# Residue-order q split straight from PSUM, and a later expected landing of transfers, in a hybrid decoder layer

## The chip, the cores and the metric

The kernel runs on one core of a Trainium2 chip. The metric is the time of one execution in device microseconds; the figure for a kernel is the median of its runs. TensorE is called PE in the rows, VectorE DVE, ScalarE ACT, GpSimd POOL, and SyncE, which issues all the DMAs of this kernel, SP. All arithmetic is fp32; a matrix product is made of three passes over operands that are each split into a high and a low part in fp32r.

## The reference

One decoder layer over 1024 tokens of width 1024. Cut to what matters here:

```python
a = rmsnorm(h, ln_pre_mix)
q, k, v, u, z = split(a @ w_in)             # 3 x 512 columns for attention, 2 x 512 for gating
attn = dilated_attention(q, k, v)           # 8 heads of 64; (window, dilation) = (128,1), (512,4), (2048,16)
sgu = spatial_gating(u, z, ...)             # chunks of 128 tokens
h = h + rmsnorm(concat(rmsnorm(attn), rmsnorm(sgu)) @ w_out)
g, up = split(rmsnorm(h) @ w_gate_up)       # 2 x 2816 columns
h = h + rmsnorm((silu(g) * up) @ w_down)
h = h + sigmoid(h @ w_pe_gate + b_pe_gate) * (p @ w_pe_proj)
```

In the attention q is scaled by 64 ** -0.5. A query sees the tokens of its own neighbourhood, and farther ones only at a distance that is a multiple of four, so the far part of the second half of the sequence (tokens 512 to 1023, which look back into tokens 0 to 511) splits into four residues of the position modulo four.

## The kernel before, in words

**Order of the program.** The kernel does not issue its instructions as they are written. Every operation is recorded in a graph (`Graph.call`; all share one source line in the profile, L383), priced (`price`) and put in order by `order` (line 224): a list scheduler that keeps, for each engine, a time at which it is free, and starts the earliest written operation whose inputs are ready in the plan and whose buffers are free. Buffers are of four kinds: M (4 KB a partition, 47 of them), S (2 KB, 14), T (small, 28) and P (the eight PSUM banks, with limits by group: three for scores, two for the weighted sums, two for transposes, two for fill work). For PE an input from another engine counts as sure only after a margin of 0.25 us. Reads of a PSUM bank are ordered like writes, so two engines never read one bank at once. The instructions are then issued in the picked order, and each engine runs its own list in that order. A DMA is planned at lines 326 to 331: it starts 0.4 us after its issue or when the one before has moved its bytes, takes its bytes at 330 KB per us (`load` has a `rate` that divides this, for transfers in small pieces), ends a fixed time later, and no more than eight are in flight.

**Stages.** The products use a two-level block scheme of seven block products (`in_products`; numbers 1, 2, 6, 5, 3, 7, 4 in this order for q and k). In order of time: norm and transposes of x with the V projection, then z and u with the gating unit, then q and k, to about 221.5 us; attention for four pairs of heads, first half and then second half of the sequence, mixed with fill work (the output projection of the gating part, the p embeddings, and the first two block products of 20 column blocks of the feed-forward: `gated`, `ple`, `first_products`), to about 475; the rest of gate/up, the down projection and the last gate, to the end.

**Around the change.** After block product 2, four PSUM banks hold, added to what product 1 left, q of the first half of the sequence, feature-major: 128 features (two heads) by 512 tokens. After product 4, the last, the four banks hold q of the second half. `q_out` (line 763) scales a bank into a high part (ScalarE `mul`) and a low part (VectorE `scalar_tensor_tensor`: scaled source minus high part), both in one M tile, and stores it to DRAM (`q_low`, `q_high`). For the second half it also makes a copy `turned` in which the 512 tokens are regrouped by residue modulo four: two ScalarE copies, one of each part, which read the M tile at a step of four elements and write it contiguously; a second DMA stores it as `q_far`. The attention loads these back with the two heads stacked differently: `stacked_q` (line 807), `prepare_low` (line 813, six loads a pair) and `prepare_high` (line 820, twelve loads a pair). `prepare_high` for a pair is recorded behind step 2 of the pair before, and for the first pair in the last pair's first half.

`far_unit` makes the scores of the four residues, a softmax, transposes and a weighted sum for one head; its ScalarE copy out of the `av` bank reads PSUM at a step of 128 elements. `unit` does the same for a pair of near query blocks. In both, `softmax` is a VectorE pass that adds the bias and takes the row maximum (CUSTOM_DVE_ANT_0 in the rows), then a ScalarE exponential.

Of the kernel before, what the change touches and what calls it, by code (L numbers as in the profile page):

```python
# [12 lines left out]
F32R = mybir.dt.float32r  # L13
# [4 lines left out]
P = 128  # L18
# [5 lines left out]
HD = 64  # L24
# [8 lines left out]
LO, HI = slice(0, 512), slice(512, 1024)  # L33
ADD, SUB, MUL = ALU.add, ALU.subtract, ALU.mult
# [79 lines left out]
class Graph:  # L114
# [109 lines left out]
    def order(self):  # L224
# [19 lines left out]
        port, dma, table, lanes = 0.0, 1.5, 0, [0.0] * 8  # L244
# [37 lines left out]
        def pick(e, now):  # L282
            best = None
            front = ops[first]
            for rank, i in waiting[e][: self.LOOK[e]] + [(front.rank, first)] * ((front.rank, first) in waiting[e]):
                o = ops[i]
                if o.port[e] and port > now + 1e-9:
                    continue
                if best is not None and o.sure > now:
                    continue  # L290
                if not fits(o, now):
                    continue
                if e != "tensor" or o.sure <= now:
                    return o
                best = o
            return best
# [6 lines left out]
        while left:  # L303
            if not events:
                raise ValueError(f"stuck at {ops[first].what} {first}")
            now = heapq.heappop(events)
            while events and events[0] <= now + 1e-9:
                heapq.heappop(events)
            while coming and coming[0][0] <= now + 1e-9:
                _, rank, i, e = heapq.heappop(coming)  # L310
                if ops[i].start is not None:
                    continue
                bisect.insort(waiting[e], (rank, i))
            for e in engines:
                if at[e] > now + 1e-9 or not waiting[e]:
                    continue
                o = pick(e, now)
                if o is None:
                    continue
                busy, took = o.cost[e]  # L320
                o.start, o.engine = now, e
                picked.append(o)
                if o.table and o.table != table:
                    busy, took, table = busy + 1.4, took + 1.4, o.table
                at[e] = now + busy
                if e == "sync":
                    dma = max(dma, now + 0.4) + o.bytes / 330e3
                    o.end = dma + 1.7
                    lanes = lanes[1:] + [o.end]
                    at[e] = max(at[e], lanes[0])  # L330
                else:
                    o.end = now + took
                if o.port[e]:
                    port = o.end
                    heapq.heappush(events, port)
                for x in o.engines:
                    if (o.rank, o.i) in waiting[x]:
                        waiting[x].remove((o.rank, o.i))
                o.new = [b for b in o.bufs if b.slot is None]
                for b in o.new:  # L340
                    b.slot = heapq.heappop(free[b.kind])[1]
                    group[b.group] = group.get(b.group, 0) + 1
                    b.ahead = first
                    early[b.kind][first : b.born] += 1
                for b in o.bufs:
                    b.left -= 1
                    b.until = max(b.until, o.end)
                    if not b.left:
                        heapq.heappush(free[b.kind], (b.until, b.slot))
                        group[b.group] -= 1  # L350
                        live[b.kind][b.born : b.last + 1] -= 1
                        early[b.kind][b.ahead : b.born] -= 1
                        heapq.heappush(events, b.until)
                done[o.i] = True
                left -= 1
                while first < n and done[first]:
                    first += 1
                for u in o.users:
                    u.waits -= 1
                    if not u.waits:  # L360
                        release(u)
                heapq.heappush(events, at[e])
                heapq.heappush(events, now + 0.02)
# [25 lines left out]
def hybrid_block(ctx: ExitStack, tc, a, out):  # L389
    G = Graph()  # L390

    def M(dt=F32, shape=(P, 1024), group=None):
        return G.buf("M", shape, dt, group)
# [13 lines left out]
    def DR(shape):  # L407
        return G.buf("D", shape)
# [4 lines left out]
    def dve(what, **kw):  # L413
        return G.call("vector", what, **kw)

    def load(dst, src, rate=1.0):
        o = G.call("sync", "dma_start", dst, src)
        o.bytes /= rate
        return o

    def tt(dst, x, y, op=ADD, engines="vector"):
        return G.call(engines, "tensor_tensor", out=dst, in0=x, in1=y, op=op)

    def copy(dst, src):
        return G.call("scalar", "copy", dst, src)
# [174 lines left out]
    x = a["x"][0]  # L600
# [137 lines left out]
    for q, banks in in_products(2048, 1536, zu_mm):  # L738
        for i in range(4):
            if q in (1, 6, 5):  # L740
                v, t = {1: (zs, i), 6: (us, i), 5: (us, i + 4)}[q]
# [5 lines left out]
            else:  # L747
                v = {2: zs, 3: us}.get(q, us)[i + 4 * (q == 7)]
# [10 lines left out]
    q_low, q_high, q_far = ([DR([P, 2, 512]) for _ in range(4)] for _ in range(3))  # L759
    k_all = [DR([P, 2, S]) for _ in range(4)]  # L760
    q_part, k_part = [SM() for _ in range(4)], [M(F32, (P, 2, 512)) for _ in range(4)]

    def q_out(src, dsts):
        hl = M(F32R, (P, 2, 512))
        G.call("scalar", "mul", hl[:, 0], src, HD**-0.5)
        dve("scalar_tensor_tensor", out=hl[:, 1], in0=src, scalar=HD**-0.5, in1=hl[:, 0].f32(), op0=MUL, op1=SUB)
        load(dsts[0], hl.f32())
        if len(dsts) > 1:
            turned = M(F32R, (P, 2, 512))
            for j in range(2):  # L770
                copy(turned[:, j].split(P), hl[:, j].f32().then(lambda v: v.rearrange("p (s c) -> p c s", c=4)))
            load(dsts[1], turned.f32())

    def k_out(src, cs, i):
        hl = M(F32R, (P, 2, 512))
        split(hl[:, 0], hl[:, 1], src)
        load(k_all[i][:, :, cs], hl.f32())
# [5 lines left out]
    for q, banks in in_products(0, AW, qk_mm, (1, 2, 6, 5, 3, 7, 4)):  # L783
        for i in range(4):
            dst = {1: q_part[i], 2: q_part[i], 6: k_part[i][:, 0], 3: k_part[i][:, 0], 5: k_part[i][:, 1],
                   7: k_part[i][:, 1], 4: None}[q]
            if q in (1, 6, 5):
                copy(dst, banks[i])
            elif q != 4:
                tt(dst, banks[i], dst)  # L790
            if q == 2:
                q_out(dst, [q_low[i]])
            if q == 4:
                q_out(banks[i], [q_high[i], q_far[i]])
            if q in (3, 7):
                k_out(dst, LO if q == 3 else HI, i)

# [4 lines left out]
    HALVES = slice(0, HD), slice(HD, P)  # L802

    def heads_of(v):
        return v.then(lambda u: u.rearrange("(h d) n -> d h n", d=HD))

    def stacked_q(src):
        both = M(F32R, (P, 2, 512))
        for x, rows_ in enumerate(HALVES):
            load(both[rows_].f32(), heads_of(src[:, x, :]))  # L810
        return both[:, 0], both[:, 1]

    def prepare_low(pr):
        q, k = stacked_q(q_low[pr]), [M(F32R, (P, 2, 512)) for _ in range(2)]
        for x in range(2):
            for rows_ in HALVES:
                load(k[x][rows_].f32(), heads_of(k_all[pr][:, x, LO]))
        qk[pr] = [(q[hh], k[0][:, hh], k[1][:, hh]) for hh in range(2)]

    def prepare_high(pr):  # L820
        q, qf, k = stacked_q(q_high[pr]), stacked_q(q_far[pr]), [[M(F32R) for _ in range(2)] for _ in range(2)]
        for hh in range(2):
            for x in range(2):
                for rows_ in HALVES:
                    load(k[hh][x][rows_].f32(), k_all[pr][HALVES[hh], x, :])
        qk[pr] = [(q[hh], *k[hh], qf[hh]) for hh in range(2)]


# [155 lines left out]
    p, wpp = a["p"][0][0], []  # L984
# [197 lines left out]
    def rows_out(*ts):  # L1182
        for t in ts:
            attn_out(t)
            h_chain(t)

    prepare_low(0)
    for pr in range(4):
        nxt = (lambda: prepare_low(pr + 1)) if pr < 3 else (lambda: prepare_high(0))
# [36 lines left out]
    for q in ORDER:  # L1226
        if q in (2, 5):
            two = [PB() for _ in range(4)]
        banks = two if q in (2, 5, 3) else one
        for g in range(NG):  # L1230
# [6 lines left out]
            s = winograd_b(q, lambda j, c: w_raw[g, j][:, c * 512 : (c + 1) * 512], tmp)  # L1237
# [10 lines left out]
        for i in range(4):  # L1248
            low, high = acc[i], acc[4 + i]
            dst = {1: low[:, LO], 2: low[:, LO], 6: low[:, HI], 3: low[:, HI],  # L1250
                   5: high[:, HI], 7: high[:, HI], 4: high[:, LO]}[q]
# [90 lines left out]
```

## Time and profile before

| | |
|---|---|
| median of 3 runs | 1191.13 us (1191.04 to 1193.01) |
| profiled execution | 1191.37 us, span 1189.2 us |
| mean granted TensorE clock | 0.993 |
| TensorE matmul, busy | 1170.6 us, 98% |
| VectorE, busy | 866.3 us, 73% |
| ScalarE, busy | 580.4 us, 49% |
| DMA | 208.78 MB, 176 GB/s over the span |

Busy times are of one engine and can overlap with those of the others. A row of groups gives the operation, its output and input tiles by kind (m, s, t, p are the buffers above, d is DRAM, c a constant), the shape, a count, the busy time, the mean of one in ns, and the idle time before it with what ended it. [...]

### The profile page before, as it was taken

The page shows a single profiled execution, that of the slowest core. Times are in us where ns is not written, and L with a number is a line of the kernel's source. Part 1 is how long each engine was busy: PE and PEld are TensorE (multiplying, and loading weights), DVE is VectorE, ACT ScalarE, POOL GpSimd, SP SyncE. Part 2 cuts the span into 40 slices and gives each one's busy share as a digit, 9 for nine tenths or more (in the row PEclk, how much of TensorE's full clock was granted, in tenths as well). Part 3 has the DMA queues.
Part 4 walks back from the last instruction along what each step waited for, and adds up shares of the span by engine and source line. Part 5 has one row for each costly group of instructions (what it writes and reads, how often), then busy time and mean ns, then how long its engine had stood idle before and what let it go on. Part 6 is the DMA issues. An engine that isn't in the chain of part 4 may idle for free.

```text
span 1189.2 us, 16376 instructions
## 1 busy us (share of the span) xinstructions
PE 1170.6 (98%) x5633; PEld 977.4 (82%) x5633; DVE 866.3 (73%) x1699; ACT 580.4 (49%) x1304; POOL 54.7 (5%) x68
## 2 busy tenths in 40 slices
PE   8999999899999999999999999999999999999998
PEld 6887888788888888888888888888888888888887
DVE  7888895456566566799988888887668965469643
ACT  8664335688768566667223232232344445358121
POOL 3001000000021000120000000000000000002000
PEclk9999999899999899999999999999999999999999
DMA  8214046999752996468456665545297333653111
GB/s 301 74 69 142 36 153 206 312 280 336 236 178 77 255 249 187 130 207 288 151 168 192 190 192 174 187 155 177 97 350 278 98 98 102 232 179 142 45 45 54
DMA packets 161245, 208.78 MB, mean 176 GB/s; under 512 B 12477, under 2 KB 89609, under 8 KB 161162
## 3 DMA queue, kind: packets, MB, share of 16 engines
q1 hardware_dynamic: 161162, 207.74, 55.1%
q8 instruction: 44, 0.72, 0.3%
q14 instruction: 39, 0.32, 0.1%
HBM read 147.63 MB, written 60.06 MB: 175 GB/s over the span
## 4 chain that ended last, share of the span: by engine, by line
PE 88%; DMA 5%; DVE 3%; ACT 3%; issue 0%; SPq 0%; POOL 0%; DVEq 0%; ACTq 0%
PE p L383 88%; ACT m L383 2%; DVE s L383 2%; DMA s<-d 1%; DMA m<-in_w_gate_up 1%; DVE m L383 1%; DMA m<-d 1%; DMA d<-s 1%; DMA m<-in_w_in 1%; DVE t L383 1%; ACT s L383 0%; DMA m<-in_c_bias 0%; SPq L383 0%; POOL m L383 0%; ACT L383 0%
## 5 line engine op out<-in xcount | busy, mean ns | idle before, releaser
L383 PE MATMUL p<-m,m 128*128 128x512 f32 (+2 forms) x4620 | 1071.5, 389 | 4.8 <-DMA m<-d 1.6
L383 PEld LDWEIGHTS p<-m,m 128*128 128x128 f32 x4620 | 849.9, 189 | 173.4 <-DVE m L383 3.1
L383 DVE TENSOR_TENSOR m<-m,m 128x512 fp32r<-128x512 f32 (+2 forms) x465 | 312.3, 704 | 70.4 <-ACT m L383 64.8
L383 ACT CAST m<-m 128x512 fp32r<-128x512 f32 x371 | 221.0, 633 | 193.0 <-PE p L383 152.6
L383 DVE TENSOR_TENSOR s<-p,s 128x512 f32<-128x512 f32 (+4 forms) x222 | 142.8, 654 | 88.2 <-PE p L383 52.1
L383 ACT ACTIVATE s<-s 128x512 f32<-128x512 f32 (+1 forms) x71 | 44.2, 626 | 222.9 <-DVE s L383 169.2
L383 DVE TENSOR_TENSOR m<-p,m 128x256 fp32r<-128x256 f32 (+3 forms) x132 | 61.1, 490 | 36.1 <-PE p L383 21.9
L383 POOL TENSOR_TENSOR t<-t,c 128x1 f32<-128x1 f32 (+1 forms) x56 | 39.7, 715 | 1025.8 <-ACT t L383 848.6
L383 ACT COPY s<-p 128x512 f32<-128x512 f32 (+1 forms) x122 | 62.1, 519 | 48.4 <-PE p L383 47.1
L383 ACT CAST m<-s 128x256 fp32r<-128x256 f32 (+1 forms) x121 | 53.7, 480 | 30.1 <-PE p L383 14.8
L383 DVE TENSOR_TENSOR s<-s,s 128x512 f32<-128x512 f32 x88 | 60.6, 692 | 4.9 <-ACT s L383 0.7
L383 DVE TENSOR_TENSOR m<-s,m 128x256 fp32r<-128x256 f32 (+1 forms) x121 | 58.1, 508 | 6.5 <-ACT m L383 6.5
L383 PE MATMUL p<-c,m 128*128 128x128 f32 x328 | 50.6, 282 | 4.1 <-ACT m L383 4.1
L383 PEld LDWEIGHTS p<-c,m 128*128 128x128 f32 x328 | 40.6, 145 | 10.3 <-ACT m L383 5.1
L383 PE MATMUL p<-s,m 128*128 128x128 f32 (+1 forms) x256 | 44.9, 279 | 0.8 <-ACT s L383 0.8
L383 PE MATMUL p<-c,s 128*128 128x128 f32 (+2 forms) x249 | 42.7, 282 | 1.9 <-DVE s L383 1.9
L383 ACT COPY m<-p 128x512 f32<-128x512 f32 (+1 forms) x72 | 31.3, 452 | 27.1 <-PE p L383 26.2
L383 ACT ACTIVATE m<-m 128x1024 f32<-128x1024 f32 x32 | 34.1, 1067 | 20.2 <-DVE m L383 15.9
L383 PEld LDWEIGHTS p<-s,m 128*128 128x128 f32 x256 | 39.3, 192 | 5.4 <-ACT s L383 1.7
L383 PEld LDWEIGHTS p<-c,s 128*128 128x128 f32 (+2 forms) x249 | 32.3, 146 | 11.0 <-DVE s L383 3.9
L383 DVE CUSTOM_DVE_ANT_0 m<-p,m 128x384 f32<-128x384 f32 (+2 forms) x64 | 30.1, 500 | 12.4 <-PE p L383 12.4
L383 ACT ACTIVATE m<-m,t 128x384 f32<-128x384 f32 (+2 forms) x64 | 36.8, 580 | 4.1 <-DVE t L383 3.9
(58 smaller groups left out, 513.0 us busy)
## 6 DMA issues: line engine op xcount, KB each, us to landing
d<-s SPq DMA_DIRECT2D x149, 256.0 KB, 3.0
m<-d SPq DMA_DIRECT2D x51, 512.0 KB, 4.1
m<-in_w_gate_up SPq DMA_DIRECT2D x88, 256.0 KB, 4.1
m<-d SPq DMA_DIRECT2D x87, 256.0 KB, 7.1
s<-d SPq DMA_DIRECT2D x56, 256.0 KB, 4.1
d<-m SPq DMA_DIRECT2D x28, 512.0 KB, 4.8
m<-in_w_down SPq DMA_DIRECT2D x44, 256.0 KB, 6.0
m<-in_w_in SPq DMA_DIRECT2D x20, 512.0 KB, 4.2
```

The costliest lines, as they stand in the source:

```text
L383: getattr(getattr(nc, o.engine), o.what)(*[real(v) for v in o.args], **{k: real(v) for k, v in o.kw.items()})
```

## The change

Three edits. `q_out` takes one destination and never makes `turned`. For the second half it is called twice for each bank: once for `q_high` as before, and once with a view of the same bank whose tokens are regrouped by residue, for `q_far`; its multiply and its split read PSUM at a step of four elements and write the M tile contiguously. In the ordering code the fixed time at the end of a DMA is 3.0 us instead of 1.7. And the loads of q and k for attention get a rate of 0.8, so that the ordering code expects their bytes at 264 KB per us.

```diff
@@ order()
-                    o.end = dma + 1.7
+                    o.end = dma + 3.0
@@ q_out()
-    def q_out(src, dsts):
+    def q_out(src, dst):
         hl = M(F32R, (P, 2, 512))
-        G.call("scalar", "mul", hl[:, 0], src, HD**-0.5)
-        dve("scalar_tensor_tensor", out=hl[:, 1], in0=src, scalar=HD**-0.5, in1=hl[:, 0].f32(), op0=MUL, op1=SUB)
-        load(dsts[0], hl.f32())
-        if len(dsts) > 1:
-            turned = M(F32R, (P, 2, 512))
-            for j in range(2):
-                copy(turned[:, j].split(P), hl[:, j].f32().then(lambda v: v.rearrange("p (s c) -> p c s", c=4)))
-            load(dsts[1], turned.f32())
+        hi, lo = (hl[:, x].split(P) if len(src.idx.shape) > 1 else hl[:, x] for x in range(2))
+        G.call("scalar", "mul", hi, src, HD**-0.5)
+        dve("scalar_tensor_tensor", out=lo, in0=src, scalar=HD**-0.5, in1=hi.f32(), op0=MUL, op1=SUB)
+        load(dst, hl.f32())
@@ the loop over the q/k products
-                q_out(dst, [q_low[i]])
+                q_out(dst, q_low[i])
-                q_out(banks[i], [q_high[i], q_far[i]])
+                q_out(banks[i], q_high[i])
+                q_out(banks[i].split(P).then(lambda v: v.rearrange("p a b -> p (a b)")
+                                             .rearrange("p (s c) -> p c s", c=4)), q_far[i])
@@ stacked_q(), prepare_low(), prepare_high(): all of their loads
-            load(both[rows_].f32(), heads_of(src[:, x, :]))
+            load(both[rows_].f32(), heads_of(src[:, x, :]), 0.8)
```

## Rows read from the trace of the kernel before

**Rows 1.** The page's head and its part 1: busy time, share, instructions.
```profile
span 1189.2 us, 16376 instructions
PE 1170.6 (98%) x5633; PEld 977.4 (82%) x5633; DVE 866.3 (73%) x1699; ACT 580.4 (49%) x1304; POOL 54.7 (5%) x68
```

**Rows 2.** Windows by stage: length, busy by engine, PEclk, DMA share, GB/s.
```profile
0.00:221.50 221.50, 216.46 (x993) 177.97 (x994) 175.86 (x386) 115.94 (x252) 21.26 (x27) 1.00 0.45 147
221.50:240.00 18.50, 14.67 (x71) 11.78 (x70) 10.69 (x40) 16.58 (x30) 0.00 (x0) 0.82 1.02 369
240.00:400.00 160.00, 158.53 (x936) 136.10 (x935) 99.56 (x275) 121.25 (x348) 13.95 (x19) 1.00 0.75 218
400.00:413.00 13.00, 11.36 (x63) 10.60 (x62) 7.87 (x29) 6.73 (x18) 0.00 (x0) 0.74 1.08 318
413.00:475.00 62.00, 59.98 (x354) 51.00 (x353) 39.98 (x129) 39.98 (x121) 0.00 (x0) 1.00 0.80 217
475.00:1184.80 709.80, 709.62 (x3226) 589.98 (x3224) 531.08 (x840) 279.44 (x538) 19.44 (x22) 1.00 0.50 165
1184.80:1189.20 4.40, 0.00 (x0) 0.00 (x0) 1.27 (x3) 0.42 (x1) 0.00 (x0) 0.76 0.13 45
```

**Rows 3.** Fine windows, same columns (PE, PEld, DVE, ACT, POOL), around two places.
```profile
230.00:232.00 2.00, 0.87 (x4) 0.34 (x3) 1.42 (x10) 1.98 (x3) 0.00 (x0) 0.84 0.91 285
232.00:238.00 6.00, 4.33 (x14) 3.55 (x15) 2.55 (x8) 4.54 (x13) 0.00 (x0) 0.50 1.03 415
238.00:240.00 2.00, 2.00 (x12) 1.73 (x12) 1.08 (x4) 1.59 (x5) 0.00 (x0) 0.95 1.03 420
404.00:406.00 2.00, 0.36 (x3) 0.18 (x2) 0.81 (x6) 1.33 (x5) 0.00 (x0) 0.86 1.05 314
406.00:412.00 6.00, 6.00 (x29) 6.00 (x30) 2.52 (x11) 2.67 (x6) 0.00 (x0) 0.50 1.10 360
412.00:414.00 2.00, 2.00 (x12) 1.74 (x12) 1.96 (x7) 1.67 (x7) 0.00 (x0) 0.93 1.19 214
```

**Rows 4.** The chain that ended last, 223 to 233: start us, us, what.
```profile
223.14 8.68 ACT m L383 x10
231.83 1.28 ACT L383
```

**Rows 5.** Timeline of PE, five pieces: start, us, form, count, [idle before <-releaser].
```profile
228.07 0.44 PE L383 MATMUL p<-m,m 128*128 128x128 f32 x2 [0.72 <-DVE m L383]
228.67 2.31 PE L383 MATMUL p<-m,m 128*128 128x256 f32 x8 [0.16 <-DVE m L383]
233.67 0.47 PE L383 MATMUL p<-c,m 128*128 128x128 f32 x1 [2.69 <-ACT m L383]
...
405.87 1.09 PE L383 MATMUL p<-m,m 128*128 128x128 f32 x4 [1.64 <-DMA m<-d]
...
468.90 0.33 PE L383 MATMUL p<-c,m 128*128 128x128 f32 x1 [1.25 <-ACT m L383]
```

**Rows 6.** Groups of instructions by form, 221 to 232, ACT and DVE.
```profile
L383 ACT CAST m<-m 128x512 fp32r<-128x512 f32 x8 | 8.4, 1120 | 0.0
L383 ACT ACTIVATE m<-p 128x512 fp32r<-128x512 f32 x4 | 2.3, 590 | 6.8 <-PE p L383 6.8
...
L383 DVE SCALAR_TENSOR_TENSOR m<-p,m 128x512 fp32r<-128x512 f32 x4 | 2.7, 689 | 8.7 <-ACT m L383 8.7
```

**Rows 7.** The same view over the whole span: that form of cast.
```profile
L383 ACT CAST m<-m 128x512 fp32r<-128x512 f32 x371 | 221.0, 633 | 193.0 <-PE p L383 152.6 <-DVE m L383 35.0 <-DMA m<-in_w_gate_up 2.9
```

**Rows 8.** ACT on the S tiles, 326 to 470: ns minimum/median/maximum, forms.
```profile
L383 ACT COPY s<-p x35: 349/404/601, 331.8 to 469.2; 128x256 f32<-128x256 f32 x19, 128x512 f32<-128x512 f32 x16
```

**Rows 9.** One window, the columns of rows 2.
```profile
221.00:232.00 11.00, 8.85 (x49) 6.90 (x48) 7.06 (x28) 10.46 (x13) 0.00 (x0) 0.97 1.01 333
```

**Rows 10.** DMA issues, 384 to 408: queue, count, KB each, median us to landing.
```profile
m<-d SPq DMA_DIRECT2D x13, 256.0 KB, 6.7
```

**Rows 11.** What SP waited for, 380 to 410: us in total, times, longest.
```profile
SPq L383 <- PE p L383: 12.7, 5, 8.3
```

More of the change, by code (lines that the diff above doesn't have):

```diff
@@ L816, in prepare_low @@
             for rows_ in HALVES:
-                load(k[x][rows_].f32(), heads_of(k_all[pr][:, x, LO]))
+                load(k[x][rows_].f32(), heads_of(k_all[pr][:, x, LO]), 0.8)
         qk[pr] = [(q[hh], k[0][:, hh], k[1][:, hh]) for hh in range(2)]
@@ L824, in prepare_high @@
                 for rows_ in HALVES:
-                    load(k[hh][x][rows_].f32(), k_all[pr][HALVES[hh], x, :])
+                    load(k[hh][x][rows_].f32(), k_all[pr][HALVES[hh], x, :], 0.8)
         qk[pr] = [(q[hh], *k[hh], qf[hh]) for hh in range(2)]
```

## The prediction

> **What bounds the kernel now.** First the page's head: TensorE is busy 1170.6 of 1189.2 us [rows 1], so all the idle time there is to win is 18.6 us. Next, the busy time by stage [rows 2] shows where it lies: the stage's length minus PE busy gives 5.0 us from the start to 221.5 (V projection, gating, q/k projection), 3.8 us from 221.5 to 240 where the q/k projection hands over to attention, 1.5 us from 240 to 400, 1.6 us from 400 to 413, 2.0 us from 413 to 475, 0.2 us in the whole feed-forward part (475 to 1184.8) and 4.4 us at the end. The feed-forward and the end do not contain the edited code, and neither does the first stretch but for its last product. What a change of the attention part can win in idle time is thus about 9 us. The same rows show a second loss, in the clock: the granted clock averages 0.82 and 0.74 in 221.5 to 240 and 400 to 413, and 1.00 elsewhere (the end, where PE is idle, aside).
>
> [...] The first begins at about 231.4, in a window in which PE is busy 0.87 us of 2, and ends at about 238.2: 6.8 us low, of which PE worked some 4.5 us, so about 2.3 us are lost. The second begins in the window in which PE is busy 0.36 us of 2 (404 to 406) and ends at about 412.3: 6.8 us low, some 6.4 us worked, 3.2 us lost. So place A (221.5 to 240) costs 3.8 + 2.3 = 6.1 us, and place B (400 to 413) costs 1.6 + 3.2 = 4.8 us. Everything else in attention is 3.5 us, in small pieces.
>
> Last, what ends each wait. The chain of waits [rows 4] passes at A through ScalarE: ten ScalarE pieces in a row, 8.68 us from 223.14, then its table load of 1.28 us, then the first exponentials, and only then TensorE at 233.67, whose transposes waited 2.69 us for ScalarE [rows 5]. At B the timeline [rows 5] shows four score matmuls of 128 columns with 1.64 us of idle before them, released by a DMA into an M tile: a q/k load of the far branch that landed late.
>
> **Part 1, the residue-order q at A.** Removed: eight ScalarE copies (two for each of four banks) that read SBUF at a step of four elements. In 221 to 232 there are exactly eight such casts, at a mean of 1120 ns [rows 6], where the same form over the whole kernel has 633 ns [rows 7]: the step costs 0.49 us each, and the eight take 9.0 us (8.4 us within the window). Added: four ScalarE multiplies that read PSUM at that step, and four VectorE scalar_tensor_tensor that do so too. The contiguous forms took 590 and 689 ns [rows 6].
>
> No row shows these two with a step on PSUM. For ScalarE the nearest is the far branch's own copy, which reads a PSUM bank at a step of 128 elements: it is among the 16 PSUM to S-tile copies of 512 columns, and of that whole group the longest took 601 ns [rows 8]. So the bounds are 0.59 us and 1.08 us (0.59 plus the 0.49 of a stepped SBUF read), and I take 0.59. For VectorE there is no stepped read at all: 0.69 to 1.18 us by the same surcharge; I take 0.69, since the nearest stepped read of PSUM, ScalarE's, shows no surcharge.
>
> [...]
>
> Now the order at A. The code treats reads of one bank as ordered, so each bank goes multiply, split, multiply, split, alternating ScalarE and VectorE. VectorE sets the pace: eight splits of 0.69 are 5.5 us from 222.1, to about 227.6; ScalarE's last multiply is done at about 226.9 instead of its last cast at 231.8. Behind it the table load (1.28) ends near 228.2 instead of 233.1. But the exponential also needs a row maximum from VectorE, which has these reductions queued beside the splits: VectorE was busy 7.06 us in 221 to 232 [rows 9], and 2.8 us more makes 9.8 of 11, so it now becomes the late engine. If the splits go first, the first reduction ends near 228.0, the first exponential near 228.5, and the transposes start at about 229 instead of 233.7. The banks of the product come free at about 223.5, 224.9, 226.3 and 227.6; so far the third and fourth came after the splits that released TensorE at 228.07 and 228.67 [rows 5]. TensorE's scores in 226 to 231 were spread by these waits. I take the idle time at A from 3.8 down to 1.0 us, a gain of 2.8 (bounds: 0 to 3.8), and the clock to stay up, a gain of 2.3 (bounds 0 to 2.3; the gap of 1.25 us at 468.90 [rows 5] lies in a stage at a clock of 1.00 [rows 2]). Sum for A: 5.1 us. The four DMAs of the residue q are issued earlier; the DMA engines are at a share of 1.02 there [rows 2], so they only change places with other transfers. I cost that at nothing; cover gone, one 512 KB transfer at the 369 GB/s of that row is 1.4 us.
>
> **Part 2, the expected landing.** This changes no instruction, but the order in which all engines take them. In the ordering code a load of 256 KB so far ended 0.4 + 0.8 + 1.7 = 2.9 us after its issue; now it is 0.4 + 0.8 + 3.0 = 4.2, and 4.4 for the q/k loads with their rate of 0.8. Measured around B, the median of 13 such loads is 6.7 us [rows 10]. The new figure is nearer but still short. Consumers move back 1.3 to 1.5 us in the plan and TensorE takes fill work (gated and first feed-forward products) ahead of them; the wait at B was 1.64 us. If all else stays, 0.1 to 0.3 us of it are left, without a dip: 4.8 us gained. But everything upstream is drawn anew, so whether this very wait still falls there is even odds; I take half, 2.4 us (bounds: 0 to 4.8).
>
> Against it stands the rest of the redraw: 3.5 us of small waits in attention, and the S, M and PSUM tiles that loads need. In 380 to 410 SP waited 12.7 us in five waits for PE to release a tile [rows 11]; consumers planned later hold tiles longer, and the loads behind in SP's queue (weights, biases, the next pair) start later. I take a loss of 1.5 us (bounds: a gain of 3.5, a loss of 9.6, two gaps like B). Feed-forward and end: nothing, because PE idles 0.2 us in 709.8 there and the DMA share is 0.50 [rows 2], so a load that is planned 1.3 us later is still far ahead; without that cover one gap like B, 4.8 us. The start: nothing; its first loads go out at once in any order, and one reordered load there would move it by about 1 us.
>
> Sum: 5.1 + 2.4 - 1.5 = 6.0 us. On the profiled execution (1191.37 us, span 1189.2) that is 1185.4; this execution lies 0.24 us above the median of 1191.13, so the forecast is **1185.1 us**.
>
> **The rivals.** *Both places clear.* A loses 6.1, B 4.8, and the small waits stay: 10.9 us, about 1180.2. For it: one cause each, named above, and both edits aim there. Against it: the landing in the plan is still 2.3 us short of the measured median.
>
> *VectorE takes ScalarE's place at A.* If the stepped PSUM reads pay 0.49 us on both engines, the splits end at 222.1 + 4 x 0.69 + 4 x 1.18 = 229.6, the first reduction at 230, the transposes at about 231, only 2.7 us earlier; the gap and the dip stay in part, since the plan does not know of the surcharge. A gains about 1.5, B's even odds are eaten by the redraw: 1189.6, within what counts as no change or just outside. The same number holds if the ordering code puts the second pair of reads behind other work, so that the banks are held: the change would then not do what it says.
>
> *The redraw opens new gaps.* Place: the far scores and the first scores of a pair between 240 and 475. Mechanism: tiles held longer by later consumers, so the twelve loads that prepare a pair's second half issue later, and TensorE meets one that has not landed. Price: each gap of 1.6 us brings the low clock with it, 4.8 us as at B. With one such gap beside B, A's gain is used up; from the second on the kernel is slower: 1191.1 - 5.1 + 2 x 4.8 = 1195.6. For it: the DMA engines are full (shares 1.02 and 1.08 at A and B), so order decides what lands in time. Against it: a later expected landing can only make the plan more careful, and fill work is there.
>
> **Chances.** Forecast 0.50 (its own range 1181.5 to 1188.7), both clear 0.16, VectorE or banks 0.20, new gaps 0.14. A difference of 0.2%, 2.4 us, is about what can be told from no change: under 1188.7 is faster, over 1193.5 slower. Faster: 0.48 of the forecast, 0.16, and a quarter of the VectorE case, 0.69 in all; slower: 0.14; same: the remaining 0.17. The range 1179.5 to 1192.0 leaves out most of the new gaps and the far end of both clear, some 0.2.
>
> **What would show it.** Right at A: no ScalarE casts near 1.1 us after the q/k projection; eight multiplies and eight splits there, near 0.59 and 0.69; the table load at 227 to 229; PE idle at most 1.5 us in that stage and the clock at 1.00. Wrong: splits near 1.18, or a gap before the first transposes as long as 2 us with a clock of 0.50. At B: the far scores of each pair without a wait on a DMA over 1 us. The forecast is wrong if PE's idle time from the end of the projection to the feed-forward stays at 9 us, or if dips in the clock are still two or more; it is wrong altogether if the difference comes from the feed-forward part.

## The result, and the profile after

The changed kernel takes 1178.1 us at the median of four runs (1178.0 to 1178.8), the kernel before 1191.1; the ratio is 0.9893 with an interval of 0.9875 to 0.9911. It is faster by 13 us where 6 were forecast, and 1178.1 lies under the low end of the range, 1179.5. The profiled execution has a span of 1176.2 us against 1189.2, so the 13 us can be looked for inside it.

The page's head, and what TensorE waited for in all (us in total, times, longest), in the changed kernel:

```profile
span 1176.2 us, 16341 instructions
PE 1163.5 (99%) x5633; PEld 972.4 (83%) x5633; DVE 869.0 (74%) x1703; ACT 576.3 (49%) x1300; POOL 57.0 (5%) x68
```

```profile
PE p L383 <- DVE s L383: 2.8, 3, 1.4
PE p L383 <- DVE m L383: 2.5, 4, 0.7
PE p L383 <- DMA m<-in_ln_pre_mix: 2.4, 1, 2.4
PE p L383 <- ACT m L383: 0.5, 2, 0.3
```

No wait on a q/k load (`m<-d`) is left, the kind that stood at 405.87 in [rows 5]; the one on `in_ln_pre_mix` is at the start. Against [rows 1] the idle time of PE falls from 18.6 to 12.7 us, 5.9, and its busy time by 7.1 us with the same 5633 matmuls. Most of that second part is the clock. The same stages as in [rows 2]:

```profile
0.00:221.50 221.50, 216.09 (x991) 177.49 (x992) 175.88 (x386) 116.51 (x251) 22.56 (x27) 1.00 0.45 147
221.50:240.00 18.50, 17.47 (x103) 14.64 (x102) 12.66 (x34) 14.54 (x35) 0.00 (x0) 1.00 1.03 372
240.00:400.00 160.00, 158.19 (x941) 136.00 (x940) 104.75 (x300) 121.73 (x347) 14.01 (x19) 1.00 0.79 232
400.00:413.00 13.00, 13.00 (x83) 11.40 (x82) 11.51 (x43) 10.27 (x35) 0.00 (x0) 1.00 1.08 288
413.00:470.00 57.00, 57.00 (x349) 49.40 (x348) 37.89 (x111) 39.90 (x110) 0.00 (x0) 1.00 0.79 222
470.00:1171.80 701.80, 701.74 (x3177) 583.51 (x3175) 525.03 (x829) 272.93 (x523) 20.45 (x22) 1.00 0.50 165
```

At place A (221.5 to 240) PE idles 1.03 us, where it had 3.83; at place B (400 to 413) none, where it had 1.64; and the clock, which all rows give as a share of full speed, is 1.00 in both. Two dips are gone, stretches at 0.50 in [rows 3]; the prediction priced them at 2.3 and 3.2 us, half of the some 4.5 and 6.4 us that TensorE worked in them. The small waits, 3.5 us before, are 1.8 now. So the account is 2.8 + 2.3 at A, 4.8 at B, 1.7 in small waits, 11.6 in all; the first stage idles 0.4 us longer. The remaining 1.6 us of PE busy time is not fully placed. Some of it lies in attention's small matmuls: the 80 score matmuls of 128 columns are busy 13.6 us in all, where they were 15.3. Their mean falls from 319 to 303 ns, but much of that is the dips again; the 73 that ran outside them had 310 ns. That these counted as busy while they stood alone, between short waits, is argued and not shown.

What happened at A, by form, 221 to 232 (these answer to [rows 6]):

```profile
L383 ACT ACTIVATE m<-p 128x512 fp32r<-128x512 f32 x8 | 4.4, 606 | 7.0 <-PE p L383 6.9
...
L383 DVE SCALAR_TENSOR_TENSOR m<-p,m 128x512 fp32r<-128x512 f32 x8 | 5.1, 687 | 6.5 <-ACT m L383 6.5
```

Eight multiplies, eight splits, half of each with the step of four on PSUM, and the means are within 16 ns of what the contiguous forms took (590 and 689). The casts of 1.12 us are gone, and three casts of fill work stand in this stretch, two of them between the multiplies. The timelines of VectorE, ScalarE and PE then show the first row maximum ready by 227.4, the table load 3.9 us earlier than in [rows 4], and the transposes at 230.23 instead of 233.67 with no gap before them:

```profile
227.08 0.28 DVE L383 CUSTOM_DVE_ANT_0 m<-p,m 128x128 f32<-128x128 f32 x1
```

```profile
227.97 1.28 ACT L383 ACT_TABLE_LOAD   x1
229.26 0.40 ACT L383 ACTIVATE m<-m,t 128x128 f32<-128x128 f32 x1
```

```profile
226.02 0.66 PE L383 MATMUL p<-c,s 128*128 128x128 f32 x4 [0.40 <-DVE m L383]
227.31 3.08 PE L383 MATMUL p<-m,m 128*128 128x512 f32 x13 [0.63 <-DVE m L383]
230.23 0.27 PE L383 MATMUL p<-c,m 128*128 128x128 f32 x1
```

TensorE bridges the table load with the thirteen matmuls of the second row. Such a row merges neighbours and names the shape of the first alone: by form they are nine of 512 columns, two of 384 and two of 256, so scores as well as fill work. Before, the first cast of fill work behind the hand-over came only after the stepped ones, and TensorE stood still from 230.98 to 233.67. The kernel before:

```profile
234.02 0.56 ACT L383 CAST m<-p 128x512 fp32r<-128x512 f32 x1
```

### The profile page after: what moved, and what is told of

It reads as the page before. It is cut to its first block, busy times and chain, and to the rows that moved or that the text cites. A ratio compares the mean times of both kernels' runs of the same rounds, so it can differ in the third digit from the quotient of the medians.

```text
span 1176.2 us, 16341 instructions
## 1 busy us (share of the span) xinstructions
PE 1163.5 (99%) x5633; PEld 972.4 (83%) x5633; DVE 869.0 (74%) x1703; ACT 576.3 (49%) x1300; POOL 57.0 (5%) x68
## 4 chain that ended last, share of the span: by engine, by line
PE 95%; DVE 2%; ACT 1%; DMA 1%; issue 0%; SPq 0%; POOL 0%; DVEq 0%; ACTq 0%
PE p L383 95%; DVE s L383 1%; ACT m L383 1%; DMA m<-in_w_in 1%; DVE t L383 1%; DMA d<-m 0%; DVE m L383 0%; SPq L383 0%; POOL m L383 0%; ACT s L383 0%; ACT t L383 0%; DVEq L383 0%; ACTq L383 0%
## 5 line engine op out<-in xcount | busy, mean ns | idle before, releaser
L383 ACT CAST m<-m 128x512 fp32r<-128x512 f32 x363 | 212.7, 622 | 192.8 <-PE p L383 148.1
L383 ACT CAST m<-p 128x256 fp32r<-128x256 f32 (+1 forms) x80 | 34.4, 498 | 6.7 <-PE p L383 5.7
```

What stands on the lines that cost most here:

```text
L383: getattr(getattr(nc, o.engine), o.what)(*[real(v) for v in o.args], **{k: real(v) for k, v in o.kw.items()})
```

## The experiments

Theory 1: each place has its own cause, the q edit clears A and the later landing clears B. Rival 2: the q edit does everything. Rival 3: any redraw of the order moves the gaps about, and the changed kernel's order is a lucky one. Ratios are to the kernel before, run beside it on the same chip, with their intervals.

**The parts alone.** Each is the kernel before with a part of the diff: `q_out` alone; `dma + 3.0` alone; the rate of 0.8 alone; both edits of the ordering code.

> Only the q edit; the order expects landings as before. Theory 1 (each place has its own cause): the gap at the hand-over to attention (3.8 us and a dip of the clock) goes, the gap of 1.6 us before the far scores near 405 with its dip stays: about 6 us faster, 1185, one dip left. Rival 2 (the q edit does all of it, because the work behind it only inherits the delay): both gaps go, 1178 to 1180. Rival 3 (it is the redrawn order, the edit itself is worth little): within 2 us of before, 1189 to 1193, wherever the gaps then fall.

> Only the fixed time of 3.0 in place of 1.7; the copies of q stay. Theory 1: the first gap stays with its dip (ScalarE casts near 1.12 us in front of the first exponentials), the wait on a q/k load near 405 goes: about 5 us faster, 1186. Rival 2: both gaps stay or move, 1189 to 1193. Rival 3: anything from 1183 to 1197, and gaps at other places than before.

> Only the rate of 0.8 for the q and k loads. These loads are expected 0.2 us later each and to hold the DMA engines 0.2 us longer. Theory 1: little, 1188 to 1191, the first gap as before; the wait near 405 perhaps shorter. Rival 3: as unpredictable as the others, 1183 to 1197.

> Both edits of the ordering code (3.0 and 0.8), the copies of q stay. Theory 1: the first gap stays, the second goes: 1185 to 1186, one dip left at 230 to 240. Rival 2: 1189 to 1193. If the q edit and the ordering edits add up, this and the kernel with the q edit alone together account for the 13 us.

Measured: the q edit alone 1188.1 us, 0.9986 [0.9973, 0.9998]; 3.0 alone 1186.4, 0.9962 [0.9946, 0.9978]; 0.8 alone 1190.5, 1.0003 [0.9993, 1.0013]; both ordering edits 1189.0, 0.9995 [0.9984, 1.0007]. The places fit theory 1 well. Of the times, those of the landing (1186 expected) and of the rate fit; the q edit alone (1185 expected) and both ordering edits (1185 to 1186) saved much less than it says. With the q edit alone, A and B, and the timeline of PE:

```profile
221.50:240.00 18.50, 17.47 (x104) 14.61 (x103) 12.66 (x34) 14.47 (x35) 0.00 (x0) 1.00 1.03 376
400.00:413.00 13.00, 9.73 (x56) 8.92 (x55) 6.76 (x27) 5.44 (x16) 0.00 (x0) 0.74 1.04 312
```

```profile
254.78 0.44 PE L383 MATMUL p<-c,s 128*128 128x128 f32 x2 [2.41 <-ACT s L383]
...
404.84 0.33 PE L383 MATMUL p<-m,m 128*128 128x128 f32 x1 [1.18 <-DMA m<-d]
407.27 1.09 PE L383 MATMUL p<-m,m 128*128 128x128 f32 x4 [2.10 <-DMA m<-d]
```

A is as clear as in the changed kernel. The time came back at B, where the wait on the q/k load doubled to 3.27 us, and in a new gap of 2.41 us at 254.78 with a dip of its own (clock 0.83 over 250 to 260). That gap too goes back to a load: in the timeline of ScalarE in this kernel, its in-order queue stands still for an embedding weight that the plan thought was there.

```profile
251.15 0.62 ACT L383 CAST m<-m 128x512 fp32r<-128x512 f32 x1 [1.73 <-DMA m<-in_w_pe_proj]
...
253.84 0.62 ACT L383 CAST m<-m 128x512 fp32r<-128x512 f32 x1 [0.97 <-DMA m<-in_w_pe_proj]
```

With the landing alone, and with both ordering edits, it is the mirror image, A with its dip, B without. The first pair of lines is 3.0 alone, the second both edits:

```profile
221.50:240.00 18.50, 14.69 (x75) 12.22 (x73) 10.59 (x40) 16.50 (x29) 0.00 (x0) 0.82 1.04 363
400.00:413.00 13.00, 12.61 (x84) 11.04 (x84) 8.77 (x29) 8.65 (x26) 0.00 (x0) 1.00 1.08 317
```

```profile
221.50:240.00 18.50, 14.47 (x68) 11.51 (x67) 10.23 (x39) 16.31 (x29) 0.00 (x0) 0.82 1.02 378
400.00:413.00 13.00, 11.83 (x79) 10.23 (x78) 7.87 (x24) 7.61 (x23) 0.00 (x0) 1.00 1.07 326
```

So rival 2 falls, and both causes are shown where they were put. What theory 1 lacks is the rest: the kernels save 1.4 us (the q edit), 3 to 5 (the landing), and about 0 (the rate, and both ordering edits together), not 13 between them. New gaps took part of it back: 1.11 us at 334 with 3.0 alone, 1.40 us at 437 with both ordering edits.

**Pairs with the q edit.** The changed kernel without the rate, and with 1.7 in place of 3.0:

> The q edit with 3.0; the q and k loads keep their full rate. If each place has its own cause (the hand-over by the q edit, the wait near 405 by the landing), both are clear here and 1178 to 1181 follows, the rate worth 0 to 2 us. If the full 13 us needs all three edits, a new gap over 1.5 us with its dip stands somewhere in 240 to 470 and it is 1183 to 1188.

> The q edit with the rate of 0.8; transfers still end 1.7 after their bytes. By the separate causes: the hand-over clear (idle near 1.0 us, no dip), the wait on the far q/k load near 405 stays at 1.5 to 3 us with its dip: 1185 to 1188. If any change of the order serves, it lies anywhere from 1178 to 1190.

Measured: 1184.3, 0.9956 [0.9940, 0.9971], and 1184.9, 0.9970 [0.9956, 0.9984]. Without the later landing the wait at B is there (2.32 us before the far scores at 401.57, with its dip: clock 0.81 over 395 to 413), as expected. Without the rate B has 0.34 us, but a gap opened at 285, with a dip (0.83 over 280 to 290); the timeline of ScalarE, then of PE:

```profile
283.68 0.71 ACT L383 CAST m<-s 128x256 fp32r<-128x256 f32 x2 [4.48 <-DMA s<-d]
```

```profile
285.20 0.44 PE L383 MATMUL p<-c,s 128*128 128x128 f32 x2 [2.83 <-ACT s L383]
```

Again ScalarE stands before a load, here of V, issued at 276.43 and landed 7.2 us later. So each pair of the three edits saves at most 4 to 5 us, where all three together save 13.

**Is A the stepped read, the count of copies, or the plan's price?** Both start from the kernel with both ordering edits and q copied in SBUF. One prices the stepped copies rightly in the plan. The other takes the step out, so that the tokens are not regrouped by residue, and leaves the order of every engine as it was:

```diff
-                copy(turned[:, j].split(P), hl[:, j].f32().then(lambda v: v.rearrange("p (s c) -> p c s", c=4)))
+                o = copy(turned[:, j].split(P), hl[:, j].f32().then(lambda v: v.rearrange("p (s c) -> p c s", c=4)))
+                o.cost["scalar"] = tuple(c + 0.49 for c in o.cost["scalar"])
...
-                copy(turned[:, j].split(P), hl[:, j].f32().then(lambda v: v.rearrange("p (s c) -> p c s", c=4)))
+                copy(turned[:, j].split(P), hl[:, j].f32().then(lambda v: v.rearrange("p (c s) -> p c s", c=4)))
```

> Both ordering edits, q copied in SBUF as before, but the plan now prices each of the eight stepped copies 0.49 us higher, at what they took. If the gap at the hand-over comes of ScalarE's work itself, the eight copies still stand before the first exponentials and the gap stays, 2 to 4 us with its dip: 1186 to 1190. If it comes of the plan not knowing the price, the plan now moves copies or exponentials and the gap is under 1 us without a dip: 1182 to 1184.

> Instructions and order as in the kernel with both ordering edits alone, but the eight copies of q read and write without a step, so that the far scores take their queries in the wrong order. The casts should take 0.62 us instead of 1.12, 4 us less of ScalarE before the first exponentials. If the stepped read is the cause, the gap of 2.7 us goes to under 0.5 and the dip goes: about 5 us faster than the kernel with both ordering edits, 1183 to 1184. If the count of instructions on ScalarE is the cause, the gap shrinks by a third at most and the dip stays: 1187 to 1188.

Measured: priced 1181.1, 0.9925 [0.9910, 0.9940]; without the step 1185.2, 0.9961 [0.9948, 0.9973], 4 us better than the same order with the step. In the second, the casts by form from 221 to 232, A and B, and PE at A:

```profile
L383 ACT CAST m<-m 128x512 fp32r<-128x512 f32 x8 | 4.5, 626 | 0.0
```

```profile
221.50:240.00 18.50, 16.24 (x86) 13.86 (x86) 12.47 (x45) 15.94 (x41) 0.00 (x0) 0.91 1.01 347
400.00:413.00 13.00, 10.67 (x57) 9.74 (x57) 6.97 (x24) 6.88 (x19) 0.00 (x0) 0.74 1.05 302
```

```profile
229.96 1.62 PE L383 MATMUL p<-m,m 128*128 128x128 f32 x7 [2.18 <-DMA m<-d]
```

The step is the cause of the wait on ScalarE: at 626 ns a cast, the 2.69 us are gone. (The time lies 1 us above what that theory gave.) What is late next is a q/k load, 2.18 us, and as everything runs some 4 us earlier, the far q/k load at B is late again, 2.33 us with its dip, in an order that had it covered (0.72). The priced copies leave 1.9 us idle at A with half the dip, and B clear:

```profile
221.50:240.00 18.50, 16.64 (x83) 13.23 (x82) 11.87 (x42) 17.17 (x32) 0.00 (x0) 0.91 1.02 366
400.00:413.00 13.00, 13.00 (x88) 11.43 (x87) 11.42 (x48) 10.95 (x36) 0.00 (x0) 1.00 1.07 296
```

A came out between the two expectations, the time below both. The casts still took 1.13 us each, but the last two now stand behind the first exponential. With ScalarE's work as it was, the right price alone takes the kernel with both ordering edits from 1189.0 to 1181.1 us; the changed kernel is only 3.0 us faster. With the later landing and the rate, much of the change's gain can thus be had from a plan that knows what the copies take.

**Right price without later landing, and with more.** The first is the kernel before plus the price; the second the priced kernel with 3.6 in place of 3.0.

> The kernel before with nothing changed but the price of the eight stepped copies in the plan (0.49 us more each). If the mispriced copies cause the gap at the hand-over, it shrinks from 3.8 to under 2 us here too, while the wait near 405 on the far q/k load stays, its dip too, as the landing is as before: 1184 to 1188. If the price only helps together with the later landing: 1188 to 1191.

> q copied in SBUF, the stepped copies priced at what they take, rate 0.8, 3.6. If the plan's prices are what counts and the instructions of the q edit little, this comes to within 3 us of the changed kernel: 1178 to 1181. If the q edit is needed for its own sake, the hand-over keeps a gap of 1.5 us or more with a dip: 1182 to 1186.

Measured: 1193.3, 1.0039 [1.0023, 1.0055], and 1181.5, 0.9936 [0.9921, 0.9952]. The first is outside both expectations, slower than before: A is down from 3.8 to 3.0 us with half the dip (clock 0.91 where it was 0.82), but a far load is still late (1.32 us) and waits on ScalarE of 1.67 and 0.72 us opened between 371 and 396. The second stays about 4.5 us behind the changed kernel with the same landing (1176.8, below), with 3.3 us idle at A and half a dip (0.91). So beside a right price the q edit is worth 3 us with 3.0 and 4.5 us with 3.6 for its own sake.

**Lucky order?** The changed kernel with the fixed time at 2.4, 3.6 and 4.5, with `MARGIN = 0.30` in place of 0.25, and with 3.6 and 0.30 together:

> The changed kernel with a fixed time of 2.4 in place of 3.0. If the landing time works through the waits on q and k loads (it gives the far scores more cover the later it is), a wait of 0.5 to 1.5 us near 405 is back, with a dip or without: 1180 to 1185. If every redraw of the order throws gaps at random, it is anywhere from 1178 to 1188 with gaps at other places.

> The changed kernel with 3.6. By the cover of the loads: no wait on a q or k load over 0.3 us, 1177 to 1181, small waits on ScalarE and VectorE as they fall. By random redraws: 1178 to 1188, a dip in about half of the orders.

> The changed kernel with 4.5, nearer to the 6.7 us that loads took around 400. By the cover of the loads: no waits on loads, but the plan now holds SP back (eight in flight), so 1177 to 1184. By random redraws: 1178 to 1188.

> The changed kernel with a margin of 0.30 us instead of 0.25 before the plan counts another engine's result as sure for TensorE; nothing else. No theory gives this a value of its own: it redraws the order. If the changed kernel's gain is the sum of its two causes, 1177 to 1181, hand-over and far loads clear. If its order is a lucky draw, 1181 to 1187, with a gap over 1.5 us and a dip in 240 to 470.

> The changed kernel with 3.6 and a margin of 0.30, the two that came out at 1176.8 and 1177.0 by themselves. Little is left to win: 1175.5 to 1178.5 if their small waits were taken away together; by chance of another redraw up to 1181.

| fixed time, margin | median us | ratio, interval |
|---|---|---|
| 1.7 (the pair above) | 1184.9 | 0.9970 [0.9956, 0.9984] |
| 2.4 | 1186.5 | 0.9978 [0.9965, 0.9991] |
| 3.0 (the changed kernel) | 1178.1 | 0.9893 [0.9875, 0.9911] |
| 3.6 | 1176.8 | 0.9897 [0.9880, 0.9914] |
| 4.5 | 1179.2 | 0.9913 [0.9898, 0.9928] |
| 3.0, 0.30 | 1177.0 | 0.9902 [0.9883, 0.9921] |
| 3.6, 0.30 | 1177.2 | 0.9906 [0.9891, 0.9922] |

Five different orders with the q edit, the rate and a landing of 3.0 or more lie within 2.5 us of each other, none with a dip in attention in its profiled execution (clock 1.00 from 221.5 to 470). (Another execution with a margin of 0.30 took 1180.0 us at a mean clock of 0.997.) With a margin of 0.30, A and then all the rest of attention:

```profile
221.50:240.00 18.50, 17.48 (x104) 14.61 (x103) 12.65 (x34) 14.26 (x35) 0.00 (x0) 1.00 1.02 372
240.00:470.00 230.00, 228.43 (x1373) 197.26 (x1372) 154.85 (x458) 170.83 (x490) 14.27 (x19) 1.00 0.79 231
```

So it is no lucky draw, and rival 3 falls for this family. Below 3.0 it does not fall: the order with 2.4 came out no better than the one with 1.7. It keeps a gap of 1.44 us at 328 with half a dip (clock 0.91 over 320 to 340), which ends on VectorE behind a pass of 1.28 us over 128x1024, and one of 1.04 us at 405, which ends on ScalarE; neither was traced to a load. The kernels at 3.6 and 0.30 are not clearly better than the changed one: their intervals overlap.

**What the rate does.** The changed kernel without the rate; first with 4.0 for all transfers, then (with 3.0) with the eight loads of V alone expected 3.0 us later, then with all bytes at 264 KB per us:

```diff
-                    o.end = dma + 3.0
+                    o.end = dma + 4.0
...
-                    o.end = dma + 3.0
+                    o.end = dma + 3.0 + getattr(o, "late", 0.0)      # load_v: o.late = 3.0
...
-                    dma = max(dma, now + 0.4) + o.bytes / 330e3
+                    dma = max(dma, now + 0.4) + o.bytes / 264e3
```

> The q edit, 4.0 as the fixed time, no rate of 0.8. If the gaps that are left in the kernel with the q edit and 3.0 (1184) are loads that land later than the plan thinks, a later expected landing closes them without the rate: 1176 to 1180, no dip. If the rate itself is what matters, a gap over 1.5 us and a dip are left and it is 1182 to 1187.

> The q edit with 3.0 and no rate (1184), where ScalarE waited 4.48 us for a load of V (issued at 276.4, landed 7.2 us later) and TensorE then 2.83 us near 285 with a dip. New: the plan expects the eight loads of V 3.0 us later than other loads; nothing else. If that load is the cause, the gap near 285 and its dip go and it is 1178 to 1181. If the gap there is another load's or the whole plan's, one of 1.5 us or more stays between 240 and 300 and it is 1182 to 1187.

> The q edit with 3.0, and the plan moves all bytes at 264 KB per us in place of 330, not only those of the q and k loads (the changed kernel's rate of 0.8 gives these the same 264). If what the rate does is to tell the plan that the DMA engines are full between 225 and 325, this does it too: no wait over 1.5 us between 240 and 300, 1177 to 1181. If it matters that only q and k are slower, 1182 to 1187.

Measured: 1183.0, 0.9950 [0.9932, 0.9967]; 1179.6, 0.9900 [0.9873, 0.9927]; 1182.6, 0.9930 [0.9911, 0.9950]. The later fixed time does not replace the rate: its order still has ScalarE waiting 4.76 us for a load of V and PE 3.18 us at 282. Pricing the V loads alone gives most of it (its interval holds the changed kernel's 0.9893), but the cause is only partly cleared: no dip (clock 1.00 over 240 to 300), yet a gap remains in the same place,

```profile
284.95 0.56 PE L383 MATMUL p<-s,m 128*128 128x256 f32 x3 [2.04 <-DVE s L383]
```

and ScalarE still waited 4.6 us for such loads between 240 and 300, 2.52 us of it up to 283.04, just ahead of this gap. (The profiled execution was the slowest of the four, 1181.6; the fastest took 1177.8.) The lower speed for all bytes has no gap over 1 us there, as its theory said, but waits of up to 0.8 us elsewhere, and its time lies in the range of the other theory. How far off the plan is can be read from the DMA issues of 240 to 300 in the changed kernel (count, KB, median us from issue to landing):

```profile
m<-d SPq DMA_DIRECT2D x20, 256.0 KB, 7.5
s<-d SPq DMA_DIRECT2D x3, 256.0 KB, 6.8
```

The plan gives such a q/k load 4.4 us. The DMA engines are at a share of 1.03 in this stretch; from 475 to 1170, at 0.50, seven `m<-d` loads of the same size took 2.6 us at the median. That landing grows here with the bytes queued ahead is the author's reading and not shown; in the plan a rate adds up over the loads, a fixed time does not. That this is why the rate is needed is argued, not shown: the last of the three runs should then have come out as well as the changed kernel, and did not. What exactly the rate does stays open.

## Why the prediction was right or wrong

- **Bound and places.** Right. The gain lies in attention: idle time and clock at A and B, next to nothing in the feed-forward part.
- **The price of the q edit at A.** Right in size: idle 1.0 us forecast, 1.03 measured; no dip; stepped PSUM reads at 606 ns (multiplies, with their contiguous half) and 687 ns (splits), the low ends of the bounds; VectorE sets the pace of the splits, seven of them in one row from 222.72, and the 0.40 and 0.63 us that TensorE still idles both end on it. One part of the order at A was wrong: VectorE is not the late engine for the exponentials. The first row maximum is ready by 227.4, while ScalarE reaches its table load behind three fill casts of 0.6 us and ends it at 229.25, not near 228.2; the transposes start at 230.23, not at 229. That costs nothing, because TensorE has work there, so that the match of 1.0 and 1.03 us is in part luck.
- **The surcharge weighed there.** The prediction's upper bounds gave the multiplies and splits the 0.49 us of a stepped SBUF read. With the step of four elements on PSUM in half of them, these rows, 606 and 687 ns against 590 and 689, show no surcharge near that on ScalarE or VectorE. For SBUF the 0.49 us is borne out once more by the copies without the step, 626 against 1120 ns.
- **Part 2 is the step that failed: "I take half, 2.4 us", and "I take a loss of 1.5 us" for the redraw.** The working at B was right: it left 0.1 to 0.3 us of the wait and no dip if all else stays, and 0.39 us without a dip are left with the landing alone, 0.34 with the q edit and the landing. The even odds on it and the loss were mis-sized. In the changed kernel B was worth its whole 4.8 us, and the redraw brought no loss but a gain of 1.7 us in small waits, with 1.6 us of PE busy time that is not fully placed. That is 2.4 + 1.5 + 1.7 + 1.6 = 7.2 us, and with 0.4 us lost in the first stage, the 7 us that the forecast was short. The rival "both places clear" (10.9 us) was the right case and still 2 us short.
- **Why it failed.** The prediction treated the redraw as noise around each cause. The runs show that most gaps are not noise: at A and B, at 254.78 with the q edit alone, at 285 and 282 without the rate, they came from a load or a copy that the plan had too early. (The gaps with 2.4, and the new ones with the price alone, were not followed to one.) The stretches behind A inherit an error of the plan at A (4 us of ScalarE), so one mended error alone moves the work into the next: the q edit alone won 5.1 us at A and gave most of it back at B and at 254.78; the copies without the step saved 4 us and met a late q/k load at A and another at B. All mended together left few late inputs, and the gain is 13 us where the parts alone give 1.4, 3 to 5 and none, and the pairs at most 4 to 5.
- **Against "a later landing can only make the plan more careful".** Right for 3.0 to 4.5 with the rate. It does not hold by itself: both ordering edits without the q edit won nothing, and with the q edit and the rate 2.4 was no better than 1.7.

## What to carry to other kernels

When the order is made by a planner, a change's gain need not be the sum over its places, as it was not here: look at each gap for what the plan had too early, and ask whether the edit mends that error or only moves it to the next late load. Mend the prices of the stepped copies and of the transfers together, and test the order's luck by a neutral redraw (here the margin). Where TensorE is the bound, price a gap with its clock: in the profiled execution B cost 1.6 us in idle time and 3.2 in clock.

## What the hardware showed that was not expected

In the changed kernel ScalarE and VectorE read PSUM at a step of four fp32 elements at about the price of a contiguous read: of the eight multiplies and eight splits of 512 columns, half with the step, none took over 0.64 and 0.69 us (contiguous 0.59 and 0.69). ScalarE's stepped read of SBUF cost 1120 ns in the kernel before, against 626 in the copies without the step. And a gap of PE does not settle the clock by its length: 1.64 us at 405 came with 0.50 in [rows 3], while in the kernel with the V loads priced the gap of 2.04 us at 285 stood in a stretch whose clock stayed at 1.00:

```profile
240.00:300.00 60.00, 56.81 (x353) 48.60 (x352) 38.57 (x133) 45.51 (x134) 0.55 (x1) 1.00 1.02 292
```

Nor does the order settle it. The ten executions of the kernel with the q edit and the rate had mean granted clocks from 0.996 to 1.000, and those of the kernel before from 0.993 to 0.998. The profiled execution of the first, with its dip at B, had 0.997. So what a dip costs is read here from the one execution that was profiled, and another execution of the same kernel can be without it.
